# Pair products of two gated recurrences, in sets of 32 keys on the quarters of the array

## The chip, the core and the metric

The kernel runs on one core of a Trainium2 chip. Four engines of the core work side by side and wait for one another over semaphores: TensorE (PE: matrix products, with the weight load shown as PEld), VectorE (DVE), ScalarE (ACT) and GpSimd (POOL). The DMA engines bring weights in and take results out; SyncE (SP) issues most of the DMAs. Matrix products land in tiles of PSUM, from which DVE and ACT read them. The metric is the device time of one execution in microseconds. The median of three runs of the kernel before is 925.21 us (924.53 to 926.5).

## What is computed

One layer of a recurrent decoder, for a prompt of 512 tokens and for 8 samples of 4 tokens, 544 rows in all. A wide input projection feeds three token mixers. Two of them, GLA (key width 48, value width 96) and HGRN2 (64 and 64), are gated linear recurrences with four heads and have the same form; the third (mLSTM) isn't touched here. Then come merge gates, an output projection, two LayerNorms and an MLP. The part that matters here is the recurrence:

```python
b = jnp.cumsum(gc, axis=1)
rel = jnp.exp(jnp.where(causal, b[:, :, None] - b[:, None, :], -jnp.inf))
att = jnp.sum(qc[:, :, None] * kc[:, None, :] * rel, axis=-1)      # att[t, s], s <= t
o_intra = jnp.einsum("btsh,bshv->bthv", att, vc)
s_new = jnp.exp(b_last)[..., None] * s + jnp.einsum("bshk,bshv->bhkv", kc * jnp.exp(b_last[:, None] - b), vc)
```

`att` needs exp(b_t - b_s) for each key channel on its own, so it isn't one product of two matrices. The kernel makes it by levels: pairs (s, t) whose places lie in the two halves of the same block of 2m tokens, for m = 64, 32, 16, 8, 4, 2, 1. For one level the reference point of b is the last token of the first half, so both exponents are at most zero, and the level is a plain product of scaled keys (first halves) with scaled queries (second halves). The diagonal s = t is the plain product q.k.

## The kernel before, in words

Weights and activations of the large projections are split in two fp32r parts, high and low, and each projection is three products (`gemm`, `mm`; matmuls at L170, tile `g`, 128 rows of output by 272 tokens). Weights come as `raw` tiles by SP; ACT makes the high part `wh` (L153), DVE the low part `wl` (L154).

`gated` runs once for GLA (tiles `qg`, `kg`, `bg`, `gvt`) and once for HGRN2 (`qh`, `kh`, `bh`, `hvt`). Inside, `levels(u)` makes `att` for the prompt's first 256 tokens (u = 0), the next 256 (u = 1) and the 32 sample tokens (u = 2, levels m = 2 and 1 alone). In u = 0 and 1 there are C = 2 chunks of R = 128 tokens. The array `at` has 128 keys on the partitions and, for each of the 4C = 8 pairs of chunk and head, 128 queries. Step by step:

- Diagonal: POOL multiplies `qk`, four matmuls `dps` (L381: 128 tokens, two heads at a time) sum over the key channels, DVE copies the sums to `dsb` (L384), and eight ACT instructions `at` (L388) write a whole 128 x 128 array each, zero but for the diagonal.
- Each level: DVE subtracts the reference (`E`, L403), ACT takes two exponentials (L404, L405), DVE multiplies keys into `ke` (L407) and queries into `qe` (L414, two instructions). Then four matmuls `lv` (L422; one for each chunk and pair of heads) take all 128 keys of a chunk as weights and stream 2 x 64 queries. They are plain fp32, and each is two records in the trace. Of the 128 x 512 results most belong to keys and queries of different blocks; DVE writes the wanted ones into `at` with a predicated copy under `lmask` (L426).
- Then ACT and DVE make `P` and `W`, POOL multiplies `W` by the keys, PE transposes it (`ktp`, L444), ACT copies it (`kt`, L448).

`chunk(u, c)` uses `at` as weights for `o` (L482), adds the state's part (`o`, L485), makes the new state (`kvp`, L490; DVE `S`, L498), then norms the rows (`rms_rows`: ACT `sq` and `ss`, DVE `ss` L308 and `on` L312), and `finish_rows` transposes them (`oT`, L298) and multiplies into the gate (`ggate` or `hgate`, L300). `sample()` does the same for the samples, with matmuls `ol` (L513), `ox` (L527) and `kvs` (L534). `ox` writes 32 partitions at a time, with j = 0 to 3 choosing the quarter of the partitions.

A scheduler (`schedule_with_timeline_sim`) orders the instructions of each engine from the program's text and its own estimate of times; each engine then runs its list in order. So projections that the text puts later (`gates`, `products` of a Merge, `feed_tokens`) stand between the steps of the recurrence. PSUM tiles of the recurrence come from a pool of four (`psr`). `open_kq` makes the buffers of `gated`, which POOL clears (L849).

Of the kernel before, what the change touches and what calls it, by code (L numbers as in the profile page):

```python
# [42 lines left out]
def build(tc, I, O):  # L43
    nc = tc.nc
    with ExitStack() as ctx:
# [317 lines left out]
        def gated(q, k, b, sc, dv, vtok, sname, nt, gate):  # L363
# [5 lines left out]
            def levels(u):  # L369
# [9 lines left out]
                for c in range(C):  # L379
                    for p in range(2):  # L380
                        nc.tensor.matmul(dps[0:R, c * 4 + p * 2:c * 4 + p * 2 + 2], qk[:, p, c * R:(c + 1) * R], headsel,  # L381
                                         start=(c == 0 and p == 0), stop=(c == C - 1 and p == 1))
                dsb = t1.tile([128, 8], F32, tag="dsb", name="dsb")
                nc.vector.tensor_copy(dsb[0:R, 0:4 * C], dps[0:R, 0:4 * C])  # L384
                at = kqp.tile([128, 8, 128], F32, tag="at", name="at", bufs=2)
                atv = at[0:R, 0:4 * C, 0:R]
                for j in range(4 * C):
                    nc.scalar.activation(out=at[0:R, j, 0:R], in_=ident[0:R, 0:R], func=AF.Copy, scale=dsb[0:R, j:j + 1])  # L388

                for li, m in enumerate(LEVELS):  # L390
# [27 lines left out]
                    H = R // 2  # L418
                    for c in range(C):
                        for p in range(2):  # L420
                            o = (c * 2 + p) * 2 * H
                            nc.tensor.matmul(  # L422
                                lv[0:R, o:o + 2 * H].rearrange("p (a b) -> p a b", a=2),
                                Kv[:, p, c * R:(c + 1) * R], Q[:, p, :, c * H:(c + 1) * H],
                                start=(c == 0 and p == 0), stop=(c == C - 1 and p == 1))
                    nc.vector.copy_predicated(  # L426
                        atv.rearrange("p h (n m) -> p h n m", m=2 * m)[:, :, :, m:2 * m],
                        lmask[0:R, li, 0:H].rearrange("p (n m) -> p n m", m=m)[:, None].to_broadcast([R, 4 * C, nr, m]),
                        lv[0:R, 0:4 * C * H].rearrange("p (h n m) -> p h n m", h=4 * C, m=m))
# [414 lines left out]
        def open_kq():  # L844
            st, kqp = pool("kq", 1, "right")
            ke = [kqp.tile([128, 2, 256], F32, name=f"ke{i}") for i in range(2)]
            qe = [kqp.tile([128, 2, 2, 128], F32, name=f"qe{i}") for i in range(2)]
            for t in ke + qe:
                nc.gpsimd.memset(t, 0.0)  # L849
            return st, kqp, ke, qe  # L850
# [23 lines left out]
        kqs, kqp, ke, qe = open_kq()  # L874
# [85 lines left out]
        kqs, kqp, ke, qe = open_kq()  # L960
# [191 lines left out]
def _pack(v):  # L1152
# [45 lines left out]
    lmask = np.zeros((128, 7, 64), f)  # L1198
    for i, m in enumerate(LEVELS):
        j = np.arange(64)  # L1200
        lmask[:, i] = ((s[:, None] // (2 * m) == j[None] // m) & (s[:, None] % (2 * m) < m))
# [64 lines left out]
```

## Time and profile before

| | |
|---|---|
| median of three runs | 925.21 us (924.53 to 926.5) |
| the profiled execution | 923.02 us, of which the span of instructions is 921.2 us |
| PE busy | 902.4 us, 98% of the span |
| DVE busy | 574.3 us, 62% |
| ACT busy | 438.3 us, 48% |
| granted TensorE clock | 0.995 on the mean |

The stages follow one another in this order: first projections (0 to 75 us), mLSTM with projections between (to 162), feeding of GLA (to 180), the GLA recurrence with projections and merge gates between (180 to 287), feeding of HGRN2 (to 312), the HGRN2 recurrence with the rest of the merge between (312 to 420), the last merge and the output projection (to 524), the MLP (to the end).

A row of the timeline is: start, time from the first start to the last end, engine, line, operation, tiles as out<-in, for matmuls rows*columns of the array in use, shape, count. Matmuls overlap, so the rate of PE is read from starts: the start of the next row minus the start of this one. A row of groups is: busy time and mean duration of one, then idle time of the engine just before them and what ended it.

### The profile page before, as it was taken

The page shows a single profiled execution, that of the slowest core. Times are in us where ns is not written, and L with a number is a line of the kernel's source. Part 1 is how long each engine was busy: PE and PEld are TensorE (multiplying, and loading weights), DVE is VectorE, ACT ScalarE, POOL GpSimd, SP SyncE. Part 2 cuts the span into 40 slices and gives each one's busy share as a digit, 9 for nine tenths or more (in the row PEclk, how much of TensorE's full clock was granted, in tenths as well). Part 3 has the DMA queues.
Part 4 walks back from the last instruction along what each step waited for, and adds up shares of the span by engine and source line. Part 5 has one row for each costly group of instructions (what it writes and reads, how often), then busy time and mean ns, then how long its engine had stood idle before and what let it go on. Part 6 is the DMA issues. An engine that isn't in the chain of part 4 may idle for free.

```text
span 921.2 us, 17477 instructions
## 1 busy us (share of the span) xinstructions
PE 902.4 (98%) x7257; PEld 886.6 (96%) x7257; DVE 574.3 (62%) x1008; ACT 438.3 (48%) x826; POOL 49.6 (5%) x63
## 2 busy tenths in 40 slices
PE   9999999999998999999999999999999999999995
PEld 8998999999998999999999999999999999999994
DVE  5886567788697779785568755554333455444525
ACT  5395323677445875634544455442222345542305
POOL 1301230001001101000000000000000000000000
PEclk9999999999999999999999999999999999999998
DMA  7321242133321113122244222222222222222202
GB/s 267 126 70 69 62 133 83 49 102 89 127 69 41 52 54 98 56 71 86 89 146 142 81 92 92 93 92 75 87 92 92 92 90 74 90 92 92 92 1 98
DMA packets 38335, 82.87 MB, mean 90 GB/s; under 512 B 13156, under 2 KB 19332, under 8 KB 38256
## 3 DMA queue, kind: packets, MB, share of 16 engines
q1 hardware_dynamic: 25664, 73.41, 24.6%
q10 hardware_dynamic: 12528, 8.33, 3.2%
q8 instruction: 57, 0.93, 0.4%
q14 instruction: 22, 0.18, 0.1%
q0 software_dynamic: 64, 0.02, 0.0%
HBM read 76.51 MB, written 5.09 MB: 89 GB/s over the span
## 4 chain that ended last, share of the span: by engine, by line
PE 97%; DVE 2%; ACT 1%; issue 0%; ACTq 0%; DVEq 0%
PE g L170 83%; PE lv L422 3%; PE g L92 3%; PE o L482 1%; PE qkp L701 1%; PE oT L298 0%; PE o L485 0%; PE vt L271 0%; PE kvp L490 0%; PE m L1017 0%; PE na L743 0%; ACT merged L1140 0%; PE wps L64 0%; PE dps L381 0%; PE sp L718 0%; PE kvm L754 0%
## 5 line engine op out<-in xcount | busy, mean ns | idle before, releaser
L154 DVE TENSOR_TENSOR wl<-raw,wh 128x1024 fp32r<-128x1024 f32 (+2 forms) x139 | 154.8, 1113 | 136.9 <-ACT wh L153 136.0
L153 ACT ACTIVATE wh<-raw 128x1024 fp32r<-128x1024 f32 (+2 forms) x139 | 133.3, 959 | 200.9 <-PE g L170 169.3
L170 PE MATMUL g<-xh,wl 128*128 128x272 f32 x752 | 161.1, 291 | 0.0
L170 PE MATMUL g<-xh,wh 128*128 128x272 f32 x752 | 159.8, 291 | 0.3 <-DVE z L863 0.3
L170 PE MATMUL g<-xl,wh 128*128 128x272 f32 x752 | 157.0, 289 | 0.0
L170 PEld LDWEIGHTS g<-xh,wh 128*128 128x128 f32 x752 | 118.7, 189 | 1.8 <-DVE z L863 0.5
L170 PEld LDWEIGHTS g<-xh,wl 128*128 128x128 f32 x752 | 119.0, 188 | 1.1 <-issue 0.2
L170 PEld LDWEIGHTS g<-xl,wh 128*128 128x128 f32 x752 | 118.4, 188 | 0.1
L170 PE MATMUL g<-x1l,wh 128*128 128x272 f32 (+1 forms) x512 | 106.7, 289 | 0.0
L170 PE MATMUL g<-x1h,wh 128*128 128x272 f32 (+1 forms) x512 | 106.4, 289 | 0.0
L170 PE MATMUL g<-x1h,wl 128*128 128x272 f32 (+1 forms) x512 | 106.3, 289 | 0.0
L170 PEld LDWEIGHTS g<-x1l,wh 128*128 128x128 f32 x512 | 81.3, 189 | 0.1
L170 PEld LDWEIGHTS g<-x1h,wh 128*128 128x128 f32 x512 | 81.0, 189 | 0.0
L170 PEld LDWEIGHTS g<-x1h,wl 128*128 128x128 f32 x512 | 80.9, 188 | 0.0
L1070 ACT ACTIVATE relu<-relu,gw 128x544 f32<-128x544 f32 x32 | 24.0, 750 | 78.9 <-DVE relu L1069 78.9
L170 PE MATMUL g<-hidl,wh 128*128 128x272 f32 x280 | 58.2, 289 | 0.0
L170 PE MATMUL g<-hidh,wh 128*128 128x272 f32 x280 | 58.1, 288 | 0.0
L170 PE MATMUL g<-hidh,wl 128*128 128x272 f32 x280 | 58.0, 288 | 0.0
L170 PEld LDWEIGHTS g<-hidl,wh 128*128 128x128 f32 x280 | 44.1, 189 | 0.0
L170 PEld LDWEIGHTS g<-hidh,wh 128*128 128x128 f32 x280 | 44.0, 188 | 0.0
L170 PEld LDWEIGHTS g<-hidh,wl 128*128 128x128 f32 x280 | 44.0, 188 | 0.0
L170 PE MATMUL g<-hdw,wh 128*128 128x272 f32 x168 | 34.8, 289 | 0.0
(399 smaller groups left out, 1633.6 us busy)
## 6 DMA issues: line engine op xcount, KB each, us to landing
raw<-in_wff SPq DMA_DIRECT2D x64, 512.0 KB
raw<-in_win SPq DMA_DIRECT2D x47, 512.0 KB
raw<-in_wout SPq DMA_DIRECT2D x8, 512.0 KB
xr<-in_xT SPq DMA_DIRECT2D x15, 272.0 KB
out_yT<-merged SPq DMA_DIRECT2D x8, 272.0 KB
fw<-in_wfirst ACTq DMA_DIRECT2D x7, 256.0 KB
raw<-in_wup_ml SPq DMA_DIRECT2D x8, 192.0 KB
raw<-in_wup_gla SPq DMA_DIRECT2D x8, 192.0 KB
```

The lines of the kernel that those rows point to most:

```text
L92: nc.tensor.matmul(first_ps[i][hf], w[:, i * 128:(i + 1) * 128], a[:, k, hf * HT:(hf + 1) * HT], start=(k == 0 and n == 0), stop=(k == KD ...
L153: nc.scalar.activation(out=h[:, 0:n], in_=raw[:, 0:n], func=AF.Copy)
L154: nc.vector.tensor_tensor(out=l[:, 0:n], in0=raw[:, 0:n], in1=h[:, 0:n].bitcast(F32), op=ALU.subtract)
L170: nc.tensor.matmul(ps[:, hf, 0:w_], w, a(k)[:, hf * HT:hf * HT + w_], start=(k == 0 and s == 0), stop=(k == nk - 1 and s == 2))
L422: nc.tensor.matmul(lv[0:R, o:o + 2 * H].rearrange("p (a b) -> p a b", a=2), Kv[:, p, c * R:(c + 1) * R], Q[:, p, :, c * H:(c + 1) * H], st ...
L482: nc.tensor.matmul(o[:, h * dv:(h + 1) * dv], at[:, c * 4 + h, :], vtok[:, cc, h * dv:(h + 1) * dv], start=(h == 0), stop=(cc == 0 and h = ...
L701: nc.tensor.matmul(ps[0:96, hf, 0:HT], w[:, i, h, :], a[h][:, hf * HT:(hf + 1) * HT], start=(n == 0), stop=(n == 2))
L1070: nc.scalar.activation(out=r_, in_=r_, func=AF.Relu, bias=gw[:, 1:2])
```

## The change

In `levels`, for the diagonal and for every level of u = 0 and 1, the four matmuls with 128 keys as weights become matmuls with fewer keys, each writing only the partitions of its own keys. A set of keys takes only the queries of its own block. With `w` queries per head:

| level | before | now |
|---|---|---|
| diagonal | 4 matmuls, 128 weights columns, 2 streamed | 16 matmuls, 32 and 2 |
| m = 64 | 4 matmuls, 128 and 128 | 4 matmuls, 64 and 128 |
| m = 32 | 4 matmuls, 128 and 128 | 8 matmuls, 32 and 64 (on two quarters of the array) |
| m = 16 to 1 | 4 matmuls, 128 and 128 | 16 matmuls, 32 and 32 (on all four) |

Pairs that lie within one block of 32 tokens are now kept by place in that block, in a smaller tile `ar` (128 x 8 x 32), and `lmask` has 16 columns for a level in place of 64. The diagonal is one DVE product with a repeated 32 x 32 identity `identr`, which arrives with `cmask`. Levels 64 and 32 have no pairs in a 32-block; they are copied straight into `at` (DVE, and ACT for the second block of m = 32). At the end of the levels four ACT copies put the four 32-blocks of `ar` into `at`. The two `at` tiles are now cleared once by POOL, since their other places are never written. The sample tokens (u = 2) have one block of 32: their matmuls keep their shapes, and `ar` is used as it is.

```diff
+                        for g in range(R // 32):
+                            nc.tensor.matmul(dps[32 * g:32 * g + 32, c * 4 + p * 2:c * 4 + p * 2 + 2],
+                                             qk[:, p, c * R + 32 * g:c * R + 32 * g + 32], headsel,
+                                             start=(c == 0 and p == 0), stop=(c == C - 1 and p == 1))
-                dsb = t1.tile([128, 8], F32, tag="dsb", name="dsb")
-                nc.vector.tensor_copy(dsb[0:R, 0:4 * C], dps[0:R, 0:4 * C])
-                for j in range(4 * C):
-                    nc.scalar.activation(out=at[0:R, j, 0:R], in_=ident[0:R, 0:R], func=AF.Copy, scale=dsb[0:R, j:j + 1])
+                nc.vector.tensor_tensor(out=arv, in0=dps[0:R, 0:4 * C, None].to_broadcast([R, 4 * C, 32]),
+                                        in1=identr[0:R, None, :].to_broadcast([R, 4 * C, 32]), op=ALU.mult)
+                at = ats[u] if u < 2 else ar
...
+                    w = max(m, 16)
+                    M = max(m, 32)
+                    step = max(2 * m, 32)
                     for c in range(C):
                         for p in range(2):
-                            nc.tensor.matmul(
-                                lv[0:R, o:o + 2 * H].rearrange("p (a b) -> p a b", a=2),
-                                Kv[:, p, c * R:(c + 1) * R], Q[:, p, :, c * H:(c + 1) * H],
+                            for g in range(R // step):
+                                k0 = g * step
+                                nc.tensor.matmul(
+                                    lv[k0:k0 + M, (c * 2 + p) * 2 * w:(c * 2 + p + 1) * 2 * w].rearrange("p (a b) -> p a b", a=2),
+                                    Kv[:, p, c * R + k0:c * R + k0 + M], Q[:, p, :, (c * R + k0) // 2:(c * R + k0) // 2 + w],
...
+                    if m > 16:
+                        for g in range(R // step):
...
+                            if g:
+                                nc.scalar.activation(out=dst, in_=src, func=AF.Copy)
+                            else:
+                                nc.vector.tensor_copy(dst, src)
+                    else:
+                        nb = 16 // m
                         nc.vector.copy_predicated(
-                        atv.rearrange("p h (n m) -> p h n m", m=2 * m)[:, :, :, m:2 * m],
+                            arv.rearrange("p h (n m) -> p h n m", m=2 * m)[:, :, :, m:2 * m],
...
+                if u < 2:
+                    for g in range(4):
+                        gs = slice(32 * g, 32 * g + 32)
+                        nc.scalar.activation(out=at[gs, :, gs], in_=ar[gs], func=AF.Copy)
...
+            ats = [kqp.tile([128, 8, 128], F32, name=f"at{i}") for i in range(2)]
+            for t in ke + qe + ats:
                 nc.gpsimd.memset(t, 0.0)
```

The scheduler orders the new program anew, so projections stand elsewhere too. Three places on PE follow; shapes are of the output, a count of x8 is eight matmuls, and the lines of the new program are some lines further down (L172 is the old L170, L430 the old L422, L550 the old L527, L300 the old L298).

PE in GLA's first levels, where the sample's products `ox` stand among the levels' `lv`. Before:

```order
L170 MATMUL g<-xl,wh 128x272 x2
L422 MATMUL lv<-qe_2115,ke_2113 128x128 x4
L527 MATMUL ox<-Ss,qx 32x96 x8
L422 MATMUL lv<-qe_2114,ke_2112 128x128 x4
L534 MATMUL kvs<-vx,k_2169 128x384
```

Now:

```order
L172 MATMUL g<-hh,wl 128x272 x2
L430 MATMUL lv<-qe_2117,ke_2115 32x64 x8
L550 MATMUL ox<-Ss,qx 32x96 x8
L430 MATMUL lv<-qe_2116,ke_2114 32x32 x16
L557 MATMUL kvs<-vx,k_2170 128x384
```

The order is the same here; four matmuls became eight (m = 32) and sixteen (m = 16).

PE at the end of GLA's levels, from the last level of u = 1 to the transposition of a chunk's rows. Before:

```order
L422 MATMUL lv<-qe_2114,kg 128x128 x4
L444 MATMUL ktp<-ident,W 128x128 x4
L170 MATMUL g<-xh,wh 128x272
L170 MATMUL g<-xl,wh 128x272 x2
L170 MATMUL g<-xh,wl 128x272 x2
L482 MATMUL o<-gvt,at 128x96 x2
L490 MATMUL kvp<-gvt,kt 64x96 x4
L485 MATMUL o<-S,Qt 128x192
L482 MATMUL o<-gvt,at 128x96 x2
L485 MATMUL o<-S,Qt 128x192
L298 MATMUL oT<-ident,on 128x128 x3
```

Now (the first "..." stands for 28 more matmuls of `g`, the second for 14):

```order
L430 MATMUL lv<-qe_2116,kg 32x32 x16
L467 MATMUL ktp<-ident,W 128x128 x4
L172 MATMUL g<-xh,wh 128x272 x2
...
L172 MATMUL g<-xh,wh 128x272
L505 MATMUL o<-gvt,at_2119 128x96 x2
L508 MATMUL o<-S,Qt 128x192
L505 MATMUL o<-gvt,at_2119 128x96 x2
L508 MATMUL o<-S,Qt 128x192
L513 MATMUL kvp<-gvt,kt 64x96 x4
L172 MATMUL g<-xh,wh 128x272
...
L172 MATMUL g<-xh,wl 128x272 x2
L300 MATMUL oT<-ident,on 128x128 x3
```

Where 5 matmuls of `g` stood between `ktp` and `o`, 31 stand now; between `o` and `oT` there were none, and now there are `kvp` and 17 of `g`.

PE at the end of HGRN2, at the transposition of the last chunk's rows. Before:

```order
L170 MATMUL g<-xh,wl 128x272 x2
L298 MATMUL oT<-ident,on 128x128 x2
L170 MATMUL g<-hh,wh 128x272 x2
```

Now:

```order
L172 MATMUL g<-xh,wl 128x272 x2
L300 MATMUL oT<-ident,on 128x128 x2
L172 MATMUL g<-xh,wh 128x272 x2
L172 MATMUL g<-xl,wh 128x272 x2
L172 MATMUL g<-xh,wl 128x272 x2
L172 MATMUL g<-hh,wh 128x272 x2
```

Six matmuls of `g` that need nothing from the recurrence now stand between `oT` and the first product with `hh`, which is made from the finished `hgate`.

More of the change, by code (lines that the diff above doesn't have):

```diff
@@ L104, in build @@
         mf_ = wp.tile([128, 1024], F32, tag="raw", name="mf_", bufs=3)
-        nc.scalar.dma_start(out=mf_[:, 0:448], in_=I["lmask"])
-        lmask = const.tile([128, 7, 64], I32, name="lmask")
-        nc.vector.tensor_copy(lmask.rearrange("p a b -> p (a b)"), mf_[:, 0:448])
+        nc.scalar.dma_start(out=mf_[:, 0:112], in_=I["lmask"])
+        lmask = const.tile([128, 7, 16], I32, name="lmask")
+        nc.vector.tensor_copy(lmask.rearrange("p a b -> p (a b)"), mf_[:, 0:112])
         mf2 = wp.tile([128, 1024], F32, tag="raw", name="mf2", bufs=3)
-        nc.scalar.dma_start(out=mf2[:, 0:160], in_=I["cmask"])
+        nc.scalar.dma_start(out=mf2[:, 0:192], in_=I["cmask"])
         cmask = const.tile([128, 128], BF16, name="cmask")
@@ L426, in levels @@
-                    nc.vector.copy_predicated(
-                        atv.rearrange("p h (n m) -> p h n m", m=2 * m)[:, :, :, m:2 * m],
-                        lmask[0:R, li, 0:H].rearrange("p (n m) -> p n m", m=m)[:, None].to_broadcast([R, 4 * C, nr, m]),
-                        lv[0:R, 0:4 * C * H].rearrange("p (h n m) -> p h n m", h=4 * C, m=m))
+                            for g in range(R // step):
[3 more added lines that the diff above has]
+                                    Kv[:, p, c * R + k0:c * R + k0 + M], Q[:, p, :, (c * R + k0) // 2:(c * R + k0) // 2 + w],
+                                    start=(c == 0 and p == 0), stop=(c == C - 1 and p == 1))
@@ new lines, in levels @@
+                    if m > 16:
+                        for g in range(R // step):
+                            k0 = g * step
+                            src = lv[k0:k0 + M, 0:8 * w].rearrange("p (h q) -> p h q", h=8)
+                            dst = at[k0:k0 + M, :, k0 + m:k0 + 2 * m]
+                            if g:
[4 more added lines that the diff above has]
+                        nb = 16 // m
+                        nc.vector.copy_predicated(
+                            arv.rearrange("p h (n m) -> p h n m", m=2 * m)[:, :, :, m:2 * m],
+                            lmask[0:R, li, :].rearrange("p (n m) -> p n m", m=m)[:, None].to_broadcast([R, 4 * C, nb, m]),
+                            lv[0:R, 0:4 * C * 16].rearrange("p (h n m) -> p h n m", h=4 * C, m=m))
@@ L847, in open_kq @@
             qe = [kqp.tile([128, 2, 2, 128], F32, name=f"qe{i}") for i in range(2)]
-            for t in ke + qe:
+            ats = [kqp.tile([128, 8, 128], F32, name=f"at{i}") for i in range(2)]
+            for t in ke + qe + ats:
                 nc.gpsimd.memset(t, 0.0)
-            return st, kqp, ke, qe
+            return st, kqp, ke, qe, ats
         ga3 = ft.tile([128, 568], F32R, tag="ft", name="ga3")[:, 0:T]
@@ L959, in build @@
         hgate = feed_gate(M_HT, 2, V_HG, "hgate", True, rest)
-        kqs, kqp, ke, qe = open_kq()
+        kqs, kqp, ke, qe, ats = open_kq()
         gated(qh, kh, bh, 1.0, 64, hvt, "hg", 2, hgate)
@@ L1197, in _pack @@
     s = np.arange(128)
-    lmask = np.zeros((128, 7, 64), f)
+    lmask = np.zeros((128, 7, 16), f)
+    r = s[:, None] % 32
     for i, m in enumerate(LEVELS):
-        j = np.arange(64)
-        lmask[:, i] = ((s[:, None] // (2 * m) == j[None] // m) & (s[:, None] % (2 * m) < m))
+        lmask[:, i] = ((r // (2 * m) == np.arange(16)[None] // m) & (r % (2 * m) < m))
     cmask = np.where(s[:, None] <= s[None], 0.0, NEG).astype(f)
@@ L1222, in _pack @@
         wfirst=win[0:NF].reshape(NF, 128, 8, 128).transpose(2, 1, 0, 3).reshape(8, 128, NF * 128), vec=vec, gatew=gw, wqk=wqk, sel=sel,
-        ident=np.eye(128, dtype=f), lmask=lmask.reshape(128, 448), cmask=np.concatenate([cmask, sm], 1), small=small, lastsel=last,
+        ident=np.eye(128, dtype=f), lmask=lmask.reshape(128, 112), cmask=np.concatenate([cmask, sm, r == np.arange(32)[None]], 1), small=small, lastsel=last,
         gla=gla.reshape(2, 128, 8, 96), hg=hg.reshape(2, 128, 8, 64), mC=mC,
```

14 lines of the change are left out of this document (5 added, 9 removed).

## The prediction

> **What bounds the kernel now.** I read the page first, then the stages, the chain of waits, and last PE's timeline in the two stages that the change touches.
>
> ```profile
> PE 902.4 (98%) x7257; PEld 886.6 (96%) x7257; DVE 574.3 (62%) x1008; ACT 438.3 (48%) x826; POOL 49.6 (5%) x63
> PE 97%; DVE 2%; ACT 1%; issue 0%; ACTq 0%; DVEq 0%
> 180.00:300.00 120.00, 116.99 (x964) 113.29 (x963) 94.74 (x176) 73.71 (x169) 7.39 (x10) 0.99 0.26 85
> 300.00:421.00 121.00, 119.11 (x1012) 116.84 (x1011) 96.41 (x195) 73.93 (x176) 6.88 (x6) 1.00 0.22 67
> ```
>
> PE sets the end: the chain that ended last is 97% PE. In the two recurrence stages (third and fourth row: length, then busy time of PE, PEld, DVE, ACT and POOL) PE is idle for 3.0 and 1.9 us, DVE for about 25 us in each. So time can be won in two ways: shorter matmuls on PE, or fewer of its few stalls. What is taken from DVE and ACT counts only where PE waits for it. Those places:
>
> ```profile
> PE oT L298 <- DVE on L312: 2.6, 1, 2.6
> PE g L170 <- ACT hh L191: 1.9, 1, 1.9
> PE o L482 <- DVE at L426: 0.3, 1, 0.3
> 276.42 1.34 DVE at L426
> 283.00:287.00 4.00, 4.00 (x24) 3.43 (x23) 1.94 (x3) 0.49 (x1) 0.99 (x2) 0.57 0.02 4
> 418.28 0.79 DVE gb L227
> 418.00:421.00 3.00, 1.11 (x9) 0.87 (x9) 2.11 (x5) 2.31 (x5) 0.00 (x0) 1.00 0.07 22
> ```
>
> At the end of GLA, PE waits 0.3 us for the last predicated copy and 2.6 us for `on`; then the granted clock is 0.57 for 4 us, which costs 0.43 x 4 = 1.7 us: 4.6 us together. At the end of HGRN2 it waits 1.9 us for `hh`; there the clock stays at 1.00.
>
> **The matmuls of a level.** A batch's price is read from the starts of rows:
>
> ```profile
> 209.24 1.05 PE L422 MATMUL lv<-qe,ke 128*128 128x128 f32 x8
> 210.05 0.49 PE L170 MATMUL g<-xh,wh 128*128 128x272 f32 x2
> 210.38 0.42 PE L170 MATMUL g<-xl,wh 128*128 128x272 f32 x2
> 202.51 1.05 PE L422 MATMUL lv<-qe,ke 128*128 128x128 f32 x8
> 203.50 0.54 PE L527 MATMUL ox<-Ss,qx 128*32 128x96 f32 x16
> 205.24 0.54 PE L527 MATMUL ox<-Ss,qx 128*32 128x96 f32 x16
> 205.71 0.52 PE L170 MATMUL g<-xh,wl 128*128 128x272 f32 x2
> 206.06 0.41 PE L170 MATMUL g<-xh,wh 128*128 128x272 f32 x2
> 206.31 0.29 PE L170 MATMUL g<-xl,wh 128*128 128x272 f32 x1
> 330.63 0.42 PE L527 MATMUL ox<-Ss,qx 128*32 128x64 f32 x14
> 330.98 0.39 PE L170 MATMUL g<-xh,wl 128*128 128x272 f32 x1
> 312.81 0.29 PE L422 MATMUL lv<-qe,ke 128*32 128x32 f32 x4
> 312.94 0.29 PE L422 MATMUL lv<-qe,kh 128*32 128x32 f32 x4
> 364.67 0.45 PE L490 MATMUL kvp<-hvt,kt 128*64 128x64 f32 x8
> 365.05 0.39 PE L170 MATMUL g<-xh,wl 128*128 128x272 f32 x1
> 183.66 0.95 PE L381 MATMUL dps<-small,qk 128*128 128x2 f32 x8
> 184.47 0.38 PE L170 MATMUL g<-xh,wl 128*128 128x272 f32 x1
> ```
>
> Two matmuls of `g` take 0.25 us (206.06 to 206.31). A full batch of `lv` takes 0.81 us (209.24 to 210.05), and the pair of `g` behind it 0.33, so 0.89 us in all; the diagonal's `dps` takes 0.81 + 0.08 likewise. There are 28 such `lv` batches and 4 of `dps`: 28.5 us of PE.
>
> The nearest rows for the new shape are `ox` (four quarters of the array in turn) and the sample's `lv` (the same 32 x 32 form, all on one quarter). 16 records of `ox` with 96 columns take 0.47 us, 29 ns each; 14 with 64 columns take 0.35, 25 ns each. One quarter alone takes (312.94 - 312.81)/4 = 32 ns for each record of 32 columns. So `ox` with three times the columns is no slower for each record: the quarters work side by side. Taking both `ox` rows as four rounds of four, the difference of 0.12 us over 4 x 32 columns is 0.93 ns a column; a round of 32 columns is then 0.03 us, which the 32 ns of the single quarter confirm, and 0.11 us stay over as fill and drain. Going in and out has a price too: `lv` before `ox` takes 0.99 us where 0.89 is usual (202.51 to 203.50), and the pair of `g` after `ox` takes 0.35 for 0.25 (205.71 to 206.06): 0.10 + 0.10.
>
> - m = 16 to 1 (20 batches, 32 records each on four quarters). Low end: 8 rounds x 0.03 + 0.11 + 0.20 = 0.55 us. High end: 25 ns for each record as in `ox`, 0.80 + 0.20 = 1.00 us. I take 0.65, near the low end, because the spacing in `ox` falls with its columns, so columns set it and not the issue; the rest is for the fact that no row shows more than 18 such records in a row. Against 0.89: -0.24 x 20 = -4.8 us (-6.8 to +2.2).
> - m = 32 (4 batches, 16 records of 64 columns on two quarters). The row of `kvp` has 64 columns on two halves: 8 records in 0.38 us. Twice that and 0.20 is 0.96; 8 rounds x 0.06 + 0.11 + 0.20 is 0.79. I take 0.85: -0.2 us (-0.4 to +0.3).
> - m = 64 (4 batches, 8 records of 128 columns, all on one half). Nothing runs side by side, so the 0.81 stays, with 0.11 and 0.20 on top: 1.1 to 1.2. I take 1.15: +1.0 us (+0.8 to +1.2).
> - Diagonal (4 batches, 32 records of 2 columns): as m = 16, 0.55 to 1.00; 0.65 taken: -1.0 us (-1.4 to +0.4).
>
> PE's own work: -5.0 us (-7.8 to +4.1). Some batches stand beside `ox` and share the going in and out; two are split by a `kvs`. These about cancel.
>
> [...]
>
> **DVE, ACT and POOL.**
>
> ```profile
> L426 DVE COPY_PREDICATED at<-lmask,lv 128x512 f32<-128x512 int32 x28 | 25.0, 893 | 10.3 <-PE lv L422 9.1 <-ACT at L388 1.0
> L426 DVE COPY_PREDICATED at<-lmask,lv 32x64 f32<-32x64 int32 x4 | 1.2, 288 | 0.6 <-ACT at L388 0.5
> L388 ACT ACTIVATE at<-ident,dsb 128x128 f32<-128x128 f32 x32 | 10.0, 388 | 1.3 <-DVE dsb L384 1.3
> L516 ACT ACTIVATE os<-ol 32x256 f32<-32x256 f32 x1 | 0.4, 357 | 0.0
> L153 ACT ACTIVATE wh<-raw 128x1024 fp32r<-128x1024 f32 x24 | 25.3, 1055 | 18.2 <-PE g L170 17.9 <-DVE ke L407 0.2
> L849 POOL MEMSET ke<- 128x512 f32 x2 | 1.0, 528 | 8.8 <-PE lv L422 8.8
> ```
>
> The 28 large predicated copies (25.0 us) become 20 of a quarter of the size: from 64 to 512 elements the mean goes from 288 to 893 ns, 1.35 ns an element, so 128 take about 374 ns, 7.5 us. Eight plain copies come in, at most 0.6 us each, and four products of 128 x 256 for the diagonal: DVE loses some 12 us. ACT loses 32 instructions of 388 ns and takes on 20 of 32 x 256, for which 357 ns is the nearest row: -5 us. Of this nothing is counted by itself, since PE stood idle for it in the tails alone; POOL's two more clears for each recurrence come while it waits for others (8.8 us ahead of the old clears). They are twice the size of the one shown, about 1.05 us each; if that cover went, they would hold up `qk` by 2 us.
>
> **The tails.** Here the order on PE moves, and each wait is worked out anew:
>
> ```profile
> L498 DVE SCALAR_TENSOR_TENSOR S<-S,P,kvp 64x96 f32<-64x96 f32 x12 | 3.8, 313 | 3.2 <-PE kvp L490 2.9
> 280.99 0.56 DVE ss L308
> 282.14 0.57 DVE on L312
> L154 DVE TENSOR_TENSOR wl<-raw,wh 128x1024 fp32r<-128x1024 f32 x23 | 28.0, 1219 | 1.9 <-ACT wh L153 1.7
> 418.99 0.42 DVE L300 TENSOR_TENSOR hgate<-oT,hgate 128x256 f32<-128x256 f32 x1
> 419.76 0.55 ACT hh L191
> ```
>
> - GLA: `o` now has 31 matmuls of `g` ahead of it, 31 x 0.125 = 3.9 us, so the last predicated copy (and four ACT copies, 1.4 us) fit under it. `oT` has `kvp` and 17 of `g`, 2.1 us, ahead. DVE needs from the end of `kvp` four `S` (1.25), `ss` (0.56), a `wl` which now stands before `on` (1.22) and `on` (0.57): 3.6 us. What is late next is `on`, by about 1.5 us. That is less than the 1.9 us after which the clock held, so the slow clock should go too: 4.6 - 1.6 = -3.0 us (-4.6 to 0).
> - HGRN2: behind `oT` come six of `g`, 0.75 us; `hgate` (0.42) no longer stands behind a `gb` (0.79), then `hh` (0.55). With 0.3 us between, 1.3 - 0.75 = 0.5 us is left of 1.9: -1.4 us (-1.9 to 0).
> - New waits: the four ACT copies into `at` stand behind two `wh` on ACT, and behind these copies stand `kt`, which `kvp` needs, and `sq`. Two `wh` (2 x 1.06) and the copies are 3.5 us against 3.9 of cover, and `kt` comes on top. I take 0.8 us for the lot (0 to 4).
>
> The sum: -5.0 - 3.0 - 1.4 + 0.8 = -8.6 us. The profiled execution took 923.0, so it would take 914.4; the median of the runs is 2.2 us above that execution, which gives **916.5 us**.
>
> **The rivals.**
>
> 1. *The quarters go in turn, or PE can't be fed 32 short records in a row* (slower). Then a record costs the 32 ns of the single quarter: 32 x 0.032 + 0.31 = 1.33 us a batch, +0.44 on 24 batches = +10.6, +1.0 for m = 64, and for m = 32 16 x 0.06 + 0.31 = 1.27, +1.5. With the tails and new waits (-3.6) that is +9.5 us, 935. It decides from about 21 ns a record: there 24 batches at 0.98 eat up the tails. Against it: four quarters of `ox` at 25 to 29 ns with two to three times the columns. For it: the most in a row was 18. Chance 0.08. [...]
> 2. *The batch ends at its high end* (no change): PE +4.1, tails -3.6: +0.5 us, 925.7. It is the mean spacing of `ox` without its fall by columns. Chance 0.10.
> 3. *The tails only move*: the chain from `kvp` to `on` outlasts the 17 of `g` again and the clock falls again; PE's -5.0 stays, the tails give -0.5: 919.7. For it: a `wl` now stands inside the chain. Chance 0.17.
> 4. *All at the low ends*: -7.8 on PE, -5.5 in the tails, 912. Chance 0.15.
>
> **How the numbers follow.** The forecast (-8.6, with 913 to 920 as its own range) has 0.50, the rivals 0.08, 0.10, 0.17 and 0.15. The range of 910 to 925.5 holds the forecast, the third and fourth, and the better part of the second. A measurement of this kernel can tell about 0.2% (1.9 us) from no change. Faster: forecast, third and fourth, 0.82; same: the second for the most part, 0.09; slower: the first and the rest of the second, 0.09.
>
> **What would show it.** Rows of `lv` with 32 x 32 in the first stage: the next row starts 0.35 to 0.5 us after the first of x32 if the quarters overlap, 1.0 if they don't. A batch of m = 64 should still take 0.8 us or more. The wait of `oT` for `on` should be near 1.5 us with a granted clock of 1.00 right behind it, and that of `g` for `hh` near 0.5. DVE's busy time should fall by about 12 us and ACT's by 5; if the time fell by as much as these, or if PE's idle time in the two stages grew, the argument that PE sets the end would be wrong.

## The result, and the profile after

The changed kernel takes 913.26 us in the median (911.37 to 914.61), beside 925.86 us for the kernel before on the same chip: ratio 0.9864, 95% interval 0.9841 to 0.9886, so 12.6 us less. The forecast was 916.5 with a range of 910 to 925.5.

Its profiled execution took 914.61 us and is the slowest of the four, 1.4 us above their median; that of the kernel before (923.02) lies 2.8 us below the median beside it. Between the two profiles there are therefore only 8.4 us.

The page of the changed kernel: the busy times, the chain by engine, and the two recurrence stages (length, then busy time of PE, PEld, DVE, ACT and POOL, then the granted clock):

```profile
PE 893.3 (98%) x7865; PEld 872.2 (96%) x7865; DVE 563.6 (62%) x1009; ACT 435.8 (48%) x806; POOL 53.4 (6%) x67
PE 92%; DVE 3%; ACT 2%; DMA 1%; POOL 1%; issue 1%; ACTq 0%; DVEq 0%
180.00:300.00 120.00, 116.26 (x1288) 109.79 (x1287) 91.94 (x179) 76.28 (x165) 10.57 (x13) 0.97 0.28 86
300.00:421.00 121.00, 120.18 (x1363) 115.52 (x1362) 93.23 (x198) 73.16 (x165) 5.98 (x6) 1.00 0.24 71
```

PE is still 98% busy and has lost 9.1 us; DVE lost 10.7, ACT 2.5. In the GLA stage PE is now idle for 3.7 us (3.0 before) at a clock of 0.97, in the HGRN2 stage for 0.8 (1.9 before). So the time came out of PE's own work, not out of its waits.

PE's timeline at one batch of each kind (L430 is `lv`, L384 `dps`; start first):

```profile
204.03 0.41 PE L172 MATMUL g<-xh,wl 128*128 128x272 f32 x2
204.38 0.46 PE L430 MATMUL lv<-qe,ke 128*32 128x32 f32 x32
204.76 0.52 PE L172 MATMUL g<-xh,wh 128*128 128x272 f32 x2
205.12 0.41 PE L172 MATMUL g<-xl,wh 128*128 128x272 f32 x2
243.78 0.64 PE L430 MATMUL lv<-qe,ke 128*32 128x64 f32 x16
244.36 0.33 PE L300 MATMUL oT<-ident,on 128*128 128x128 f32 x1
187.76 1.09 PE L430 MATMUL lv<-qe,ke 128*64 128x128 f32 x8
188.78 0.35 PE L536 MATMUL ol<-gvt,ar 32*32 32x96 f32 x2
184.94 0.43 PE L384 MATMUL dps<-small,qk 128*32 128x2 f32 x32
185.30 0.40 PE L172 MATMUL g<-xh,wh 128*128 128x272 f32 x1
```

Start to next start, m = 16 to 1 takes 0.38 us (0.81 before), m = 32 0.58, m = 64 1.02, the diagonal 0.36 (0.81 before). The pair of `g` behind takes 0.36 where 0.25 is usual, so 0.11 us go to leaving the quarters. Going in costs nearly as much, and it stands in the row ahead: the pair of `g` takes 0.35 us to the start of the batch (204.03 to 204.38). In the kernel before, the pair ahead of the batch at 209.24 takes the usual 0.25:

```profile
208.99 0.41 PE L170 MATMUL g<-xh,wl 128*128 128x272 f32 x2
```

Taken over the whole trace, with the time of each PE instruction counted to the next start and idle time taken out, `lv` fell from 25.1 to 15.1 us and `dps` from 3.6 to 1.8: 11.8 us. Some 3 us of it went back into the rows around them: 24 of the 32 batches have a `g` right ahead, which takes 0.22 us to the start of the batch (0.125 before), 2.2 us in all, and the rest is in `kvs` and in the rows behind. About 9 us are left.

The end of GLA, with PE's waits of the whole program first:

```profile
PE oT L300 <- DVE on L314: 2.9, 1, 2.9
PE g L172 <- DVE gb L229: 0.8, 1, 0.8
PE g L172 <- ACT hh L193: 0.8, 1, 0.8
276.15 0.55 DVE L310 TENSOR_REDUCE ss<-sq 128x4 f32<-128x384 f32 x1
276.74 0.30 ACT L311 ACTIVATE ss<-ss,epsn 128x4 f32<-128x4 f32 x1 [1.97 <-DVE ss L310]
276.94 1.04 ACT L155 ACTIVATE wh<-raw 128x1024 fp32r<-128x1024 f32 x1
277.89 0.19 ACT L312 ACTIVATE ss<-ss 128x4 f32<-128x4 f32 x1
278.01 1.23 DVE L156 TENSOR_TENSOR wl<-raw,wh 128x1024 fp32r<-128x1024 f32 x1 [1.31 <-ACT wh L155]
279.27 0.56 DVE L314 TENSOR_TENSOR on<-o,ss 128x384 f32<-128x384 f32 x1
279.98 0.87 PE L300 MATMUL oT<-ident,on 128*128 128x128 f32 x3 [2.92 <-DVE on L314]
280.00:286.00 6.00, 6.00 (x29) 5.34 (x30) 3.12 (x7) 1.74 (x3) 1.85 (x2) 0.50 0.27 87
```

The wait of `oT` for `on` didn't go away, it grew from 2.6 to 2.9 us. A `wh` stands on ACT between the two small steps of `ss`, and the `wl` on DVE, which needs that `wh`, stands ahead of `on`. From 280 to 286 us, with PE at work again, the granted clock is 0.50. The same 29 records from `oT` on take 6.12 us here and 3.32 in the second profile of this kernel (experiment 7), where the clock is 1.00, so the slow clock costs 2.8 us. The end of GLA thus costs 5.7 us in this execution, 4.6 before.

### The profile page after: what moved, and what is told of

Its sections match the earlier page's. It is cut to its first block, busy times and chain, and to the rows that moved or that the text cites. A ratio compares the mean times of both kernels' runs of the same rounds, so it can differ in the third digit from the quotient of the medians.

```text
span 912.8 us, 18678 instructions
## 1 busy us (share of the span) xinstructions
PE 893.3 (98%) x7865; PEld 872.2 (96%) x7865; DVE 563.6 (62%) x1009; ACT 435.8 (48%) x806; POOL 53.4 (6%) x67
## 3 DMA queue, kind: packets, MB, share of 16 engines
q8 instruction: 62, 1.02, 0.5%
## 4 chain that ended last, share of the span: by engine, by line
PE 92%; DVE 3%; ACT 2%; DMA 1%; POOL 1%; issue 1%; ACTq 0%; DVEq 0%
PE g L172 80%; PE g L92 2%; PE lv L430 2%; PE o L505 1%; POOL cvo L634 1%; PE qkp L724 1%; PE oT L300 1%; ACT wh L155 0%; PE o L508 0%; DMA fw<-in_wfirst 0%; DVE wl L156 0%; PE kvp L513 0%; PE m L1041 0%; PE na L766 0%; ACT merged L1164 0%
## 5 line engine op out<-in xcount | busy, mean ns | idle before, releaser
L172 PE MATMUL g<-xh,wh 128*128 128x272 f32 x752 | 162.3, 293 | 0.3 <-DVE z L887 0.3
L172 PE MATMUL g<-xh,wl 128*128 128x272 f32 x752 | 158.4, 290 | 0.5 <-DVE wl L156 0.5
L172 PE MATMUL g<-xl,wh 128*128 128x272 f32 x752 | 156.7, 289 | 0.0
L172 PEld LDWEIGHTS g<-xh,wh 128*128 128x128 f32 x752 | 119.2, 189 | 2.7 <-DVE z L887 0.5
L172 PEld LDWEIGHTS g<-xh,wl 128*128 128x128 f32 x752 | 118.5, 188 | 1.4 <-DVE wl L156 0.7
L172 PEld LDWEIGHTS g<-xl,wh 128*128 128x128 f32 x752 | 118.4, 189 | 0.2
L172 PE MATMUL g<-x1l,wh 128*128 128x272 f32 (+1 forms) x512 | 106.7, 289 | 0.0
L172 PE MATMUL g<-x1h,wh 128*128 128x272 f32 (+1 forms) x512 | 106.4, 289 | 0.0
L172 PE MATMUL g<-x1h,wl 128*128 128x272 f32 (+1 forms) x512 | 106.3, 289 | 0.0
L172 PEld LDWEIGHTS g<-x1l,wh 128*128 128x128 f32 x512 | 81.3, 189 | 0.1
L172 PEld LDWEIGHTS g<-x1h,wh 128*128 128x128 f32 x512 | 81.0, 189 | 0.0
L172 PEld LDWEIGHTS g<-x1h,wl 128*128 128x128 f32 x512 | 80.9, 188 | 0.0
L172 PE MATMUL g<-hidl,wh 128*128 128x272 f32 x280 | 57.9, 288 | 0.0
L172 PE MATMUL g<-hidh,wl 128*128 128x272 f32 x280 | 57.8, 288 | 0.0
L172 PE MATMUL g<-hidh,wh 128*128 128x272 f32 x280 | 57.7, 287 | 0.0
L172 PEld LDWEIGHTS g<-hidh,wh 128*128 128x128 f32 x280 | 43.9, 188 | 0.0
L172 PEld LDWEIGHTS g<-hidh,wl 128*128 128x128 f32 x280 | 43.9, 188 | 0.0
L172 PEld LDWEIGHTS g<-hidl,wh 128*128 128x128 f32 x280 | 43.6, 188 | 0.0
L172 PE MATMUL g<-hdw,wh 128*128 128x272 f32 x168 | 34.9, 289 | 0.0
```

The source lines that it names most:

```text
L172: nc.tensor.matmul(ps[:, hf, 0:w_], w, a(k)[:, hf * HT:hf * HT + w_], start=(k == 0 and s == 0), stop=(k == nk - 1 and s == 2))
```

## The experiments

Ratios are to the kernel before, measured on the same chip in the same session, with the 95% interval.

**1. Relief of DVE and ACT alone, in the kernel before.**

```diff
-                for j in range(4 * C):
-                    nc.scalar.activation(out=at[0:R, j, 0:R], in_=ident[0:R, 0:R], func=AF.Copy, scale=dsb[0:R, j:j + 1])
+                if u < 2:
+                    nc.scalar.activation(out=at, in_=ident[:, None, :].to_broadcast([128, 8, 128]), func=AF.Copy, scale=dsb[:, 0:1])
...
-                        atv.rearrange("p h (n m) -> p h n m", m=2 * m)[:, :, :, m:2 * m],
+                        atv[:, 0:NH].rearrange("p h (n m) -> p h n m", m=2 * m)[:, :, :, m:2 * m],
```

> The kernel before, with its matmuls on PE left as they are, and only DVE and ACT relieved: the predicated copy of a level takes two of the eight pairs of chunk and head (a quarter of the elements), and the diagonal is written by one ACT instruction for each 256 tokens in place of eight, with the sums of the first head for all. So the pairs of six of the eight chunks and heads are left out of the output, and their diagonals are another head's. DVE loses about 28 x 0.52 = 14.5 us, ACT about 8 us, more than the change took from either. Theory (PE sets the end; relief counts only where PE waits for DVE or ACT, in the two tails): PE busy within 1 us of 902, and 0 to -4 us, ratio 0.996 to 1.000. Rival (a good part of the gain of 12.6 us came from DVE and ACT): -8 us or more, ratio 0.991 or below.

Measured 917.91 us, ratio 0.9929 (0.9916 to 0.9943): -6.2 us, more than the theory allowed and less than the rival asked for. The profile's first row and PE's longest wait behind the first stage, and the stretch at the end of GLA:

```profile
PE 899.7 (98%) x7257; PEld 884.5 (97%) x7257; DVE 559.6 (61%) x1008; ACT 432.6 (47%) x798; POOL 49.8 (5%) x63
PE g L170 <- DVE qh L227: 0.6, 1, 0.6
276.00:288.00 12.00, 11.41 (x99) 10.91 (x96) 8.56 (x17) 5.53 (x11) 0.99 (x2) 1.00 0.30 97
```

Both tails are gone and the clock stays at 1.00; `lv` and `dps` take what they took. The two tails cost 4.6 + 1.9 = 6.5 us before, and about that was won. But this program has another order as well: at the end of GLA 37 matmuls of `g` stand between `kvp` and the `oT` that had to wait, where none stood. So it is open here whether less work or the order did it. Experiment 2 changes the order alone.

**2. The order of the ends alone, in the kernel before, with all of DVE's and ACT's old work.**

```diff
-                on = rms_rows(128, o[:, 0:d4].rearrange("p (a b) -> p a b", a=4), dv)
+                with tc.high_priority(2 * OFF):
+                    on = rms_rows(128, o[:, 0:d4].rearrange("p (a b) -> p a b", a=4), dv)
...
-            together(chain(chunk(1, 0), chunk(1, 1)))
+            together(chunk(1, 0), chunk(1, 1))
```

> The kernel before, with its levels untouched (full array, old copies), and only the order of the ends changed: the norm of a chunk's rows ahead of the weights, and the last two chunks of each recurrence together. DVE and ACT have all of their old work. At the end of GLA the second chunk's o, which needs S, now stands right behind kvp; at the end of HGRN2 48 matmuls of g stand between oT and the first product with hh. Theory (relief_only gained its 6 us because its order hid both tails, not because DVE and ACT had less to do): the wait for on with its slow clock (4.6 us) shrinks to a wait for S of about 1.5 us, and the 1.9 us for hh go: -4 to -6 us, ratio 0.993 to 0.996. Rival (less work on DVE and ACT is what removed the tails): with the old work they stay, 0 to -2 us, 0.998 to 1.000.

Measured 919.97 us, ratio 0.9943 (0.9928 to 0.9959): -5.6 us.

```profile
PE 901.9 (98%) x7257; PEld 885.5 (96%) x7257; DVE 573.9 (62%) x1008; ACT 437.9 (48%) x826; POOL 49.0 (5%) x63
PE g L170 <- DVE qh L227: 1.4, 1, 1.4
276.00:290.00 14.00, 12.28 (x101) 11.08 (x99) 11.00 (x19) 5.07 (x11) 1.98 (x4) 1.00 0.21 74
```

DVE (573.9) and ACT (437.9) are as busy as in the kernel before, and the waits for `on` and `hh` and the slow clock are gone all the same; what is left is 1.4 us, for `qh` and not for `S` as expected. The 6 us of experiment 1 need no relief, then: another order wins them too.

**3. The records of a quarter one behind the other, in the changed kernel.**

```diff
-                    for c in range(C):
-                        for p in range(2):
-                            for g in range(R // step):
+                            for c, p, g in ([(c, p, g) for g in range(R // step) for c in range(C) for p in range(2)] if m <= 16
+                                            else [(c, p, g) for c in range(C) for p in range(2) for g in range(R // step)]):
```

> The changed kernel, with the records of m = 16 to 1 in another order: all that go to one quarter of the array stand one after another (quarter outermost), so neighbours in the queue can't run side by side. Same records, same work on DVE and ACT. Theory (the changed kernel's batch of 32 records takes 0.39 us because four quarters work side by side): a record costs 31 ns or more, as in the sample's rows on one quarter, so a batch takes 1.0 us or more, +0.6 us x 20 = +12 us on the changed kernel: ratio to before 0.998 to 1.003, and if the rest of the array's fill shows for each record (60 ns, the other sample row), +30 us, 1.02. Rival (the 0.39 us are the price of issuing 32 short records, 12 ns each, whatever quarter they go to): no change against the changed kernel, ratio 0.984 to 0.989.

Measured 921.96 us, ratio 0.9975 (0.9961 to 0.9989), some 10 us above the changed kernel's 0.9864.

```profile
206.56 0.90 PE L431 MATMUL lv<-qe,ke 128*32 128x32 f32 x32
207.39 0.52 PE L172 MATMUL g<-xh,wh 128*128 128x272 f32 x2
286.04 0.52 PE L300 MATMUL oT<-ident,on 128*128 128x128 f32 x3 [2.92 <-DVE on L314]
286.00:293.00 7.00, 6.96 (x58) 6.65 (x59) 6.03 (x11) 3.57 (x7) 1.85 (x2) 1.00 0.31 89
```

The batch takes 0.83 us, 26 ns a record (31 or more were expected, so a little less), and with the same records in the same number. That is no better than the 0.81 us on the full array: the whole gain of a level hangs on neighbours in the queue going to different quarters. Over the whole trace `lv` goes from 15.1 to 23.2 us, 8.1 of the 10. The rest is not all due to the edit: in this execution PE waits 2.4 us for `xh` near 10 us (0.6 in the changed kernel), and the granted clock is 0.57 for 4 us behind it (11 to 15 us). The wait for `on` is the changed kernel's, but the clock behind it is 1.00 here.

**4. Half the columns, twice the records, in the changed kernel.**

```diff
-                            for g in range(R // step):
+                            for g, e in [(g, e) for e in range(2 if w == 16 and u < 2 else 1) for g in range(R // step)]:
+                                v = w // 2 if w == 16 and u < 2 else w
...
-                                    Kv[:, p, c * R + k0:c * R + k0 + M], Q[:, p, :, (c * R + k0) // 2:(c * R + k0) // 2 + w],
+                                    Kv[:, p, c * R + k0:c * R + k0 + M], Q[:, p, :, (c * R + k0) // 2 + e * v:(c * R + k0) // 2 + e * v + v],
```

> The changed kernel, with each matmul of m = 16 to 1 cut in two by queries: 64 records of 16 columns for a batch in place of 32 of 32, on the quarters in the same turn; the columns in sum are the same. Theory (in the changed kernel the batch is at the price of issuing a record, 11 to 12 ns: the 32 records of the diagonal with 2 columns take 0.36 us, those of the levels with 32 columns 0.39): 0.74 us or more a batch, +0.35 x 20 = +7 us on the changed kernel, ratio to before about 0.994. Rival (columns still bound it, and the diagonal's 0.36 is fill and drain): 0.39 to 0.45 us, +0 to +1 us, 0.986 to 0.988.

Measured 918.26 us, ratio 0.9929 (0.9906 to 0.9952), about 6 us slower than the changed kernel.

```profile
223.29 0.74 PE L431 MATMUL lv<-qe,kg 128*32 128x16 f32 x64
223.96 0.37 PE L300 MATMUL oT<-ident,on 32*128 32x32 f32 x3
```

64 records take 0.67 us, 10.4 ns each: nearer to the theory's 0.74 than to the rival's 0.39 to 0.45. Read record by record from the traces, a round of four records, one on each quarter, takes 32 ns in the middle of a batch, with the 2 columns of the diagonal and with the 32 of the changed kernel's levels alike; here, with 16, it takes 31 to 35 (once in a batch about 46). The first round and the last, with the way out, add some 0.13 us (0.11 on the diagonal). So these batches are set by the number of records, and hardly by their columns; whether the issue or the quarter itself takes the 32 ns is not separated here. Of the time of the whole kernel `lv` explains 5.7 us (15.1 to 20.8); the order is another one, in which the wait for `on` is gone and others have come, with PE idle for 7.6 us in all (7.2 in the changed kernel's first profile, 7.9 in its second).

**5. m = 64 and m = 32 on all four quarters, in the changed kernel.**

```diff
+                    if m > 16:
+                        for p in range(2):
+                            for g in range(2):
+                                for c in range(2):
+                                    k0 = 32 * g if m == 64 else 64 * g
+                                    q0 = 0 if m == 64 else 32 * g
+                                    r0 = 64 * c + 32 * g if m == 64 else 32 * (2 * g + c)
+                                    nc.tensor.matmul(
+                                        lv[r0:r0 + 32, p * 2 * m:(p + 1) * 2 * m].rearrange("p (a b) -> p a b", a=2),
+                                        Kv[:, p, c * R + k0:c * R + k0 + 32], Q[:, p, :, c * 64 + q0:c * 64 + q0 + m],
...
-                            src = lv[k0:k0 + M, 0:8 * w].rearrange("p (h q) -> p h q", h=8)
-                            dst = at[k0:k0 + M, :, k0 + m:k0 + 2 * m]
+                            src = lv[r0:r0 + M, 0:4 * m].rearrange("p (h q) -> p h q", h=4)
+                            dst = at[k0:k0 + M, 4 * c:4 * c + 4, k0 + m:k0 + 2 * m]
```

> The changed kernel, with the levels m = 64 and m = 32 put on all four quarters: keys in sets of 32, the sets of the two chunks on different quarters (m = 64: 16 records of 128 columns in place of 8 on one half; m = 32: 16 records of 64 columns on four quarters in place of two); the plain copies into the array move the rows to the partitions of their keys, in halves by chunk, so DVE and ACT get 6 more instructions of half the size for each 256 tokens. Theory (batches are bound by the columns that one quarter streams, or by 12 ns a record): m = 64 takes 4 rounds x 0.107 = 0.43 to 0.55 us in place of 1.02, m = 32 0.25 to 0.35 in place of 0.57; 4 x 0.5 + 4 x 0.25 = -3 us on the changed kernel, ratio to before about 0.983 (0.981 to 0.985). Rival (sets of 32 with long streams don't run side by side, or the extra copies make PE wait): 0 to +2 us on the changed kernel, ratio 0.986 to 0.989.

Measured 912.52 us, ratio 0.9870 (0.9851 to 0.9889): the run's time can't be told from the changed kernel's.

```profile
232.30 0.65 PE L433 MATMUL lv<-qe,ke 128*32 128x128 f32 x16
232.88 1.13 PE L517 MATMUL o<-gvt,at 128*128 128x96 f32 x8
242.26 0.43 PE L433 MATMUL lv<-qe,ke 128*32 128x64 f32 x16
242.62 0.55 PE L300 MATMUL oT<-ident,on 128*128 128x128 f32 x3
PE oT L300 <- DVE on L314: 3.2, 1, 3.2
PE g L172 <- DVE qh L229: 1.4, 1, 1.4
278.00:285.00 7.00, 4.94 (x42) 4.55 (x43) 4.60 (x10) 3.28 (x7) 1.85 (x2) 1.00 0.22 78
```

The batches do what the theory said: 0.58 us for m = 64 (1.02) and 0.36 for m = 32 (0.58). Against it stand longer waits: 3.2 us for `on` (2.9) and a new 1.4 for `qh`. Together they are 1.7 us, which leaves about 1 of the 2.9 us. The profiled execution itself took 910.45 us, and the changed kernel's second one 912.66 at the same mean clock of 0.996. A gain of 1 to 2 us is below what the medians can tell.

**6. The last two chunks together, in the changed kernel** (the second edit of experiment 2).

> The changed kernel, with one word of the order changed: the last two chunks of each recurrence go together in place of one behind the other, so that the second chunk's first products are queued on PE ahead of the first chunk's transposition oT. Theory (at the end of GLA PE waits 2.9 us for on, because a wh on ACT and a wl on DVE stand inside the chain from kvp to on, and the granted clock is then 0.5 for 6.4 us, which costs 3.2): with other work ahead of oT the wait falls to 1.5 us or less and the clock holds: -3 to -5 us on the profile of the changed kernel, -1 to -4 on its median, ratio to before 0.982 to 0.986. Rival (the wait goes elsewhere: to the second chunk's o, which needs S, or to hh; or the clock falls anyway): within 1 us of the changed kernel, 0.9855 to 0.988.

Measured 914.05 us, ratio 0.9887 (0.9870 to 0.9905), not faster than the changed kernel.

```profile
PE g L172 <- ACT hh L193: 1.9, 1, 1.9
PE g L172 <- DVE gb L934: 1.2, 2, 0.9
276.00:290.00 14.00, 13.65 (x109) 13.42 (x108) 11.65 (x18) 8.95 (x17) 2.28 (x3) 1.00 0.20 55
```

At the end of GLA the theory holds: the wait for `on` is gone and the clock is 1.00. At the end of HGRN2 the rival holds: with the two chunks together there, `hh` follows right behind the last `oT`, so 1.9 us are waited for it (0.8). The 1.2 us for `gb` are new too, but stand further ahead, at 349 and 387 us.

**7. The changed kernel once more, and its norm ahead of the weights** (the first edit of experiment 2 alone).

> The changed kernel as it is, timed beside the next three. Both theories expect the ratio to the kernel before near 0.986 again (0.984 to 0.989). Its profile tells apart how steady its own tail is: if the 2.9 us wait of oT for on is set by the order of the instructions, it stands there again within 0.1 us, while the stretch of slow clock behind it may be longer or shorter or absent.

> The changed kernel, with the norm of the rows of a chunk (sq, ss, on) put ahead of the weights' wh and wl in the scheduler's order; matmuls are the same. At the end of GLA 19 matmuls of g now stand between kvp and oT (17 in the changed kernel), and at the end of HGRN2 18 between oT and the first product with hh (6). Theory (a wh on ACT and a wl on DVE inside the chain from kvp to on made the wait of 2.9 us): the chain is four S, ss, two small ACT steps and on, about 3.2 us, against 2.4 of g: the wait falls to about 0.8 us, the clock holds there, and the wait for hh goes away: -3 to -5 us on the changed kernel, ratio to before 0.981 to 0.984. Rival (weights that come later make PE wait for wh or wl elsewhere, as much as is won): within 1 us of the changed kernel, 0.985 to 0.988.

The changed kernel: 912.91 us, ratio 0.9870 (0.9847 to 0.9892). With the norm first: 908.73 us, ratio 0.9826 (0.9807 to 0.9844), 4.2 us less. The changed kernel's second profile first:

```profile
280.88 0.52 PE L300 MATMUL oT<-ident,on 128*128 128x128 f32 x3 [2.92 <-DVE on L314]
280.00:287.00 7.00, 6.12 (x52) 5.81 (x53) 5.93 (x12) 3.22 (x6) 1.85 (x2) 1.00 0.24 79
```

The wait is the same to the hundredth, so the order sets it; but the clock stays at 1.00. The 2.8 us of slow clock belong to the first execution, and not to every one of this kernel. And with the norm first:

```profile
275.56 0.30 ACT L311 ACTIVATE ss<-ss,epsn 128x4 f32<-128x4 f32 x1 [1.49 <-DVE ss L310]
275.89 0.21 ACT L312 ACTIVATE ss<-ss 128x4 f32<-128x4 f32 x1
276.13 0.56 DVE L314 TENSOR_TENSOR on<-o,ss 128x384 f32<-128x384 f32 x1 [0.25 <-ACT ss L312]
276.83 0.52 PE L300 MATMUL oT<-ident,on 128*128 128x128 f32 x3 [0.23 <-DVE on L314]
```

The two steps of `ss` now follow each other, `on` comes right behind, and 0.23 us of the 2.92 are left. Two more `g` ahead of `oT` cover 0.25 of the difference; the rest was the `wh` and the `wl` in the chain. Of the 4.2 us on the median this wait is 2.7; the 0.8 for `hh` is gone too, since 18 matmuls of `g` stand ahead of it in place of 6.

**8. Three edits together, and then DVE loaded again.** Experiment 5, the norm first, and the last two chunks together in GLA alone; then the same kernel with each predicated copy done twice:

```diff
-                        nc.vector.copy_predicated(
+                        for again in range(2 if u < 2 else 1):
+                          nc.vector.copy_predicated(
```

> Three things at once: m = 64 and 32 on all four quarters (as in four_quarters, where the batches took 0.57 and 0.31 us in place of 1.02 and 0.57, 2.9 us in all), the norm ahead of the weights, and the last two chunks of GLA together (of HGRN2 not). Theory: -2.9 us on PE and -4 us in the tails on the changed kernel, ratio to before 0.978 to 0.982. Rival (waits only move: what is won on PE is lost at the next wait): 0.984 to 0.987.

> The kernel of four_norm_together with every predicated copy of 256 tokens done twice (the second writes the same values): 20 more instructions of 0.37 us on DVE, 7.5 us, over half of what the change took from DVE. The ends of both recurrences keep nearly their order (13 and 15 matmuls of g, where 16 and 17 stood, between kvp and oT). Theory (DVE's time is worth nothing but where PE waits for it): within -1 to +2 us of four_norm_together. Rival (each us of DVE in the levels counts, as the 6 us of relief_only could be read): +5 to +8 us.

The three together: 906.68 us, ratio 0.9802 (0.9784 to 0.9820), 6.2 us faster than the changed kernel beside it (912.91). Copies twice: 907.72 us, ratio 0.9816 (0.9797 to 0.9834), 1.0 us slower than without. The first rows of the two profiles:

```profile
PE 887.0 (98%) x7897; PEld 866.0 (96%) x7897; DVE 562.4 (62%) x1013; ACT 437.3 (48%) x814; POOL 53.2 (6%) x67
```

```profile
PE 886.7 (98%) x7897; PEld 866.0 (96%) x7897; DVE 567.8 (63%) x1033; ACT 435.9 (48%) x814; POOL 53.0 (6%) x67
PE lv L433 <- DVE qe L417: 0.9, 1, 0.9
PE g L172 <- ACT hh L193: 0.8, 1, 0.8
```

5.4 us more of DVE cost 1.0 us, and PE's new waits are two, of 0.9 and 0.8 us. DVE's time counts where PE waits for it, and not by itself. What the quarters for m = 64 and 32 didn't show in the time of experiment 5 shows here: 906.39 to 906.92 us with all three edits, 908.46 to 909.51 with the norm alone (where the wait for `on` was gone already). Between these two `lv` falls from 15.1 to 12.5 us over the trace, and PE's idle time grows from 4.1 to 5.4. They also differ in GLA's last two chunks, so it is not shown that the 2 us are the quarters' alone.

**9. The last two chunks of HGRN2 together as well.**

> The kernel of four_norm_together with the last two chunks of HGRN2 together too (24 matmuls of g between the two oT, 51 behind the last). Theory (its remaining waits are 0.5 us or shorter and none stands at the end of HGRN2): no more to win there, within 1 us of four_norm_together, ratio to before 0.979 to 0.982. Rival (the second chunk's o waits for S): +1 to +2 us.

Measured 906.62 us, ratio 0.9796 (0.9778 to 0.9814): no difference from experiment 8, as the theory said. These two are the fastest kernels of the study; both keep the change and beat it by about 0.7%. Beside experiment 2, which has the same two edits of the order on the old levels, this kernel (the change and the edit of experiment 5) is 13.4 us faster in the same session (919.97 to 906.62). PE is idle for 5.2 us there and 5.1 here, and `lv` and `dps` together take 28.7 and 14.4 us: with the tails out of both kernels, the gain is PE's own work.

## Why the prediction was right, and where it was not

The time was right, inside the range and 3 us below the forecast. In part that was luck: two misses of opposite sign, on PE's own work and on GLA's tail.

- **PE sets the end; DVE and ACT count for nothing by themselves.** Right. Experiment 8 costs 1.0 us for 5.4 us of DVE, and experiment 2 removes the tails with all the old work in place. DVE's fall was forecast as 12 us (10.7 measured), ACT's as 5 (2.5). One sign that the prediction names against itself did come: the time fell by as much as DVE's busy time, 12.6 us for 10.7. By the runs that is a coincidence of sizes: the loaded DVE of experiment 8 and the equal idle times of experiments 2 and 9 speak against a common cause, and PE's idle time in the two stages together did not grow (4.9 to 4.6 us).
- **m = 16 to 1.** Right that the quarters work side by side (0.38 us a batch alternating, 0.83 in turn, experiment 3), and nearly right in the sum "8 rounds x 0.03 + 0.11 + 0.20" = 0.55: a round takes 0.032 us, the rest of the batch 0.13, going in 0.09 and going out 0.11. That is 0.59 us, so -6.0 us in place of -4.8. Too high was the 0.65 taken: the 0.10 on top, for want of a row with more than 18 such records, was not needed with 32 or even 64 in a row (experiment 4). The reason given was wrong: "columns set it and not the issue" was inferred from `ox` with 64 and 96 columns, but a round takes the same 32 ns with 2 columns as with 32. That 0.93 ns a column times 32 gives 0.03 us as well was luck.
- **m = 32, m = 64, diagonal.** With the same 0.20 for going in and out: 0.78 us for the 0.85 taken, 1.22 for 1.15, 0.56 for 0.65. By these prices all the batches together give -6.4 us, between the -5.0 that was forecast and the low end of -7.8; over the whole trace it is about -9. The step that missed this is "These about cancel", on the neighbours of the batches. Of the 32 new batches only 24 have a `g` right ahead that pays 0.09 us, and only 13 a `g` right behind that pays 0.11; an `oT` right behind, for one, pays 0.06 (its first two records take 0.27 us there, 0.22 behind a `g`).
- **GLA's tail.** Wrong. "What is late next is `on`, by about 1.5 us" left out the `wh` on ACT between the two steps of `ss` (1.04 us), for which the counted `wl` waits too: the wait is 2.9 us. Experiment 7 takes that cause away, and 0.23 us are left. The conclusion that the clock would hold, "less than the 1.9 us after which the clock held", rested on one stall of each length; the same 2.92 us stall let it fall in one execution and not in another. Forecast -3.0 us; measured +1.1 in the first profile, and -1.7 where the clock holds.
- **HGRN2's tail.** Forecast 0.5 us left, measured 0.8: -1.1 us for -1.4.
- **New waits.** 0.8 us forecast and 0.8 measured, but for `gb` and not behind the copies into `at`, where nothing was waited for. The size was luck.
- **The sum.** With the clock held in the changed kernel: PE -9, GLA -1.7, HGRN2 -1.1, `gb` +0.8, which makes -11.0. Between the medians there are 12.6 us, and 11.4 in the session of experiment 7; for the executions without a profile only mean clocks are on record (0.993 to 0.996 for the changed kernel's other three), so what the clock cost there isn't known. In the profiled pair 2.8 us of it are lost to the clock, and 1.1 us to two waits in the first 75 us, in work that the change doesn't touch:

```profile
PE g L92 <- ACT xh L81: 0.6, 1, 0.6
PE g L172 <- DVE wl L156: 0.5, 1, 0.5
```

  That leaves -7.1 for the -8.4 measured; the other 1.3 us can't be put down to a row.
- **The rivals.** The fourth gave the nearest time (912), but its tails were not at their low end, nor do the low ends of the tails add up to its -5.5 (4.6 + 1.9 = 6.5). The second fell with the batch, 0.59 us for its 1.00. The third was right about the place: the tail only moved, with the `wl` it named. The first fell with its mechanism as well: it needs 21 ns a record, and the records took 10 to 12, even with 64 in a row. Its price is near that of the records in the other order (26 ns, experiment 3), but even that kernel took 921.96 us and not 935, a little less than the kernel before.

## What to carry to other kernels

Small products on quarters of the array paid here only with neighbours in the queue on different quarters: in turn by quarter a batch took 0.83 us, alternating 0.38, on the full array 0.81. Add 0.2 us for going in and out (0.09 and 0.11 beside rows of `g`), and look for the first half of it in the row ahead. Once they alternate, use all four quarters (m = 64 took 0.58 us there and 1.02 on one half, m = 32 0.36 there and 0.58 on two quarters), and up to 32 columns count records and not columns (a round of four took 32 ns with 2 columns and with 32). When a change reorders a program, follow the chain behind each wait on every engine that it crosses, instruction by instruction, since here a copy of 1.04 us on ACT, and the `wl` that needs it, made most of a wait of 2.9 us, while 5.4 us more of DVE cost 1.0.

## What the runs showed of the hardware that was not expected

- A record on alternating quarters costs 8 ns in the middle of a batch and 10 to 12 with the ends (64 of 16 columns in 0.67 us, 32 of 2 columns in 0.36); on one quarter 26 ns (32 columns).
- A stall of PE of nearly the same length lets the granted clock fall or not. Behind 2.59 us it was 0.57 for 4 us (kernel before), behind 2.92 us 0.50 for 6 us (changed kernel, first profile), behind 2.38 us 0.57 for 4 us (experiment 3, near 10 us), and behind 2.92 us, 2.92 us and 3.2 us it stayed at 1.00 (changed kernel's second profile, experiment 3 at the end of GLA, experiment 5). What decides between the two, no run here shows. A forecast of such a stall has to carry both prices: 0, and the 1.7 us (kernel before, 0.43 x 4) to 2.8 us (changed kernel, first profile) that it cost here.
